# Half of the p products moved ahead of the first norm of a two-layer decoder kernel

## The chip, the cores and the metric

The kernel runs on one core of a Trainium2 chip. The metric is the device time of one execution in microseconds (us). TensorE (PE) does the matrix products, VectorE (DVE) and ScalarE (ACT) the elementwise work, GpSimd (POOL) small work, masks and some DMAs, SyncE (SP) issues the other DMAs. Every engine works through its own instructions in the order in which the program lists them.

## The reference

Two layers over 512 positions of 1024 channels, in float32. Each layer computes, with its own weights:

```python
h = rmsnorm(x, g_pre)
proj = h @ w_in                       # queries, keys, values, gates and merge logits of four mixers
o = four causal mixers(proj)          # sparse attention, gated convolution, stick-breaking, spatial gating
z = (o * silu(gate_paths)) @ w_branch
y = sum(sigmoid(merge_logits + b_merge) * z) @ w_out
x = x + rmsnorm(y, g_post)
x = x + (p[i] @ w_ple) * sigmoid(x @ w_ple_gate)
```

The input p[i] is 512 x 256 and w_ple 256 x 1024. The product of p with w_ple depends on inputs only. The sparse attention turns its queries and keys by rotary tables, cosines and sines of the positions, which the kernel makes once.

## The kernel before

**Products.** A float32 operand is split in two float32r halves, high (a copy on ScalarE) and low (a subtraction on VectorE), and each product is three of TensorE: high by high, high by low, low by high (`mm3`, lines 266 to 271). Weights come in 180 chunks of 128 x 1024 (some 128 x 840) in the order of use (`chunk_plan`). SP loads a chunk into one of three `raw` buffers; `split_chunk` (239) makes `wh` on ScalarE and `wl` on VectorE, in one of six pairs of buffers; then it lists the load of the chunk three further on, so that SP stops there until VectorE has freed a buffer.

**Order.** There is no automatic order: the program lists all instructions. After the start it goes in steps (`step`, 315). Each step lists the elementwise work that follows from the last ones (generators in `front`, `back`, `idle`), the splits that are due (`split_steps`, 165: up to four steps ahead of the use, as the buffers allow), and then one batch of products, mostly 24 of 512 columns. So VectorE and ScalarE work on earlier results while TensorE multiplies.

**The start** is written out by hand as the string `START` (160). For each of four tiles t of 128 positions: `s` sums the squares of x (ScalarE), `h` scales it (two small sums on VectorE, the power -1/2 on POOL, then two scalings on VectorE), `t` transposes it (eight `htr` on TensorE), `e` splits it (`hh` on ScalarE, `hl` on VectorE). `w` splits the next weight chunk, and `mtc` is the six products of tile t with chunk c of the first group, T1 (queries and keys). T1 has 96 such products. Then come the rotary tables (`make_tables`, 387), the masks, the split of two more chunks, and the steps: four `cc` steps, in whose midst the rotary work on T1 (634 to 639), its transposes `qktr` and their splits (`qT`, `kT`, 653 to 661) stand; then the `tp` products (CV), of 256 columns, of which a step has 48.

**The end of a layer.** `Y0` and `Y1` are the products with w_out. `project(0)` multiplies p with the first 512 columns of w_ple (24 products, four PSUM banks, copied out by ScalarE with a factor 0.5, 1196 to 1202), G0 are the products with the first half of w_ple_gate; `project(1)` and G1 are the second half. `use_g` (1222) applies the gate: tanh on ScalarE, then VectorE with the `ple` tile. In layer 0, the use of G1 also makes the next layer's h: it needs the row `gpre`, which takes the one buffer of the rows (347, 1263), and its transposes `htr` follow the step after.

**The memory.** PSUM has eight banks, SBUF tiles of 128 x 512 come from a pool of 25 (`T`, 194).

Of the kernel before, what the change touches and what calls it, by code (L numbers as in the profile page):

```python
# [11 lines left out]
F32 = mybir.dt.float32  # L12
F32R = mybir.dt.float32r
I32 = mybir.dt.int32
AF = mybir.ActivationFunctionType
ALU = mybir.AluOpType

L = 2
# [54 lines left out]
def chunk_plan():  # L73

    plan, step = [], 0
    for l in range(L):
        here = []

        def tgroup(name, cols, steps):
            nonlocal step  # L80
            n = tiles_of(cols)
            for c in range(KT // n):
                first, last = step, step + steps - 1
                if name in PAIRED and (l, name) != (0, "T1"):
                    first, last = step + c // 2, step + c // 2 + 2
                here.append(("t", n * cols, (name, c), first, last))
            step += steps

        def ccols(*names):
            nonlocal step  # L90
            for a in names:
                here.append(("c", KT * P, a, step, step))
                step += 1

        def both(n):
            return [(n, 0), (n, 1)]

        tgroup("T1", 512, 4)
        ccols(*both("cq"), *both("ck"))
        tgroup("CV", 256, 2)  # L100
        tgroup("T2", 420, 4)
        for c in range(2):
            ccols(("bc", c), ("bx", c), ("bb", c))
        ccols(*both("du"))
        tgroup("DV", 256, 2)
        for n in MERGES:
            ccols(*both(f"gate{n}"))
        for n in MERGES:
            for h in range(2):
                here.append(("w", 1024, (n, h), step, step + 3))  # L110
                ccols(*((f"merge{n}", dt) for dt in range(4 * h, 4 * h + 4)))
        for h in range(2):
            tgroup(f"Y{h}", 512, 4)
        for h in range(2):
            here.append(("p", 1024, h, step, step))
            step += 1
            tgroup(f"G{h}", 512, 4)
        plan.append(here)
    return plan
# [5 lines left out]
def lay_weights(w_in, w_branch, w_out, w_ple, w_ple_gate):  # L125
    parts = []

    def rows_in(a):

        return a.reshape(-1, P, a.shape[1]).transpose(1, 0, 2).reshape(P, -1)  # L130

    for l in range(L):
        for kind, n, arg, _, _ in PLAN[l]:
            if kind == "t":
                g, c = arg
                h = slice(512 * int(g[1]), 512 * int(g[1]) + 512) if g[0] in "YG" else None
                src = w_in[l][:, TGROUPS[g]] if h is None else (w_out if g[0] == "Y" else w_ple_gate)[l][:, h]
                r = P * tiles_of(src.shape[1])
                a = rows_in(src[r * c:r * c + r])
            elif kind == "c":  # L140
                g, c = arg
                cols = CCOLS[arg] if arg in CCOLS else _span("merge", D * int(g[5]) + P * c, P)
                a = rows_in(w_in[l][:, cols])
            elif kind == "w":
                a = rows_in(w_branch[l][arg[0]][:, 512 * arg[1]:512 * arg[1] + 512])
            else:
                a = rows_in(w_ple[l][:, 512 * arg:512 * arg + 512])
            assert a.shape == (P, n)
            parts.append(np.ascontiguousarray(a).reshape(-1))
    return np.concatenate(parts)  # L150
# [6 lines left out]
STICKD, SELECT0, ATTEND0, RATES = 3, 8, 5, (1, 2, 3, 2)  # L157


START = ("s0 h0 t0 w e0 m00 s1 h1 w t1 m01 e1 s2 h2 m10,11 t2 w e2 s3 h3 m02,12,20,21 t3 w e3 "  # L160
         "m22,03,13,23,30,31,32,33")
HOP, PE, STEP, SUMS = "hop", "pe", "step", "sums"


# [16 lines left out]
def hybrid_kernel(ctx: ExitStack, tc: tile.TileContext, w, x, p_t, pos, inv_freq, rows, small, ws_t, b_sp, out):  # L181
# [12 lines left out]
    def T(name, shape=(P, 512), dt=F32):  # L194
        return tpool.tile(list(shape), dt, tag="t", name=name)
# [21 lines left out]
    def bank(name):  # L217
        return psum.tile([P, 512], F32, tag="ps", name=name)

    def load(dst, src):  # L220
        nc.sync.dma_start(dst, src)
        return dst
# [8 lines left out]
    def load_to(i):  # L231
        while state["load"] < min(i, len(chunks)):
            k = state["load"]
            n = chunks[k][1]
            raws[k] = stream.tile([P, 1024], F32, tag="raw", name=f"raw{k}", bufs=RAWB)
            load(raws[k][:, :n], bass.AP(tensor=w.tensor, offset=w.offset + offs[k], ap=[[n, P], [1, n]]))
            state["load"] += 1

    def split_chunk(k):
        n = chunks[k][1]  # L240
        h = stream.tile([P, 1024], F32R, tag="wh", name=f"wh{k}", bufs=WB)
        lo = stream.tile([P, 1024], F32R, tag="wl", name=f"wl{k}", bufs=WB)
        halves[k] = (h, lo)
        load_to(k + 1)
        r = raws.pop(k)
        A.copy(h[:, :n], r[:, :n])  # L246
        yield HOP
        V.tensor_tensor(lo[:, :n], r[:, :n], h[:, :n].bitcast(F32), op=ALU.subtract)  # L248
        load_to(k + 1 + RAWB)

    def due(late):
# [7 lines left out]
    def take(n=1):  # L259
        k = state["use"]  # L260
        state["use"] += n
        for c in chunks[k:k + n]:
            assert c[3] <= state["step"] + n
        return list(range(k, k + n))

    def mm3(ps, a, b, start, stop):

        (ah, al), (bh, bl) = a, b
        nc.tensor.matmul(ps, ah, bh, start=start, stop=False)  # L269
        nc.tensor.matmul(ps, ah, bl, start=False, stop=False)  # L270
        nc.tensor.matmul(ps, al, bh, start=False, stop=stop)  # L271
# [15 lines left out]
    def split(h, lo, src, scale=None):  # L287
        half_h(h, src, scale)
        yield HOP
        half_l(h, lo, src, scale)  # L290
# [52 lines left out]
    def load_x(t):  # L343
        for hf in range(2):
            xin[t, hf] = load(T(f"x0_{t}_{hf}"), x[t * P:(t + 1) * P, hf * 512:(hf + 1) * 512])
# [5 lines left out]

    line = spool.tile([1, D], F32, tag="row", name="line", bufs=1)
    load(line, bass.AP(tensor=rows.tensor, offset=rows.offset, ap=[[0, 1], [1, D]]))
    load_x(0)
    lift = consts.tile([1, P], F32, name="lift")
    V.memset(lift, 1.0)
    gpre = [bank(f"gpre{k}") for k in range(2)]
    for k in range(2):
        nc.tensor.matmul(gpre[k], lift, line[:, 512 * k:512 * k + 512], start=True, stop=True)
    load_to(1)  # L360
    prms = [load(consts.tile([P, 40], F32, name=f"prm{l}"), small[l]) for l in range(L)]
    for k in range(1, NT):
        load_to(k)
        load_x(k)
    posi = consts.tile([P, NT], I32, name="posi")
    nc.gpsimd.dma_start(posi, pos)
    freq = consts.tile([P, 48], F32, name="freq")
# [180 lines left out]

    xdram = dram.tile([S, D], F32, name="xdram")


    new_hT()

# [23 lines left out]
    def split_next(n=1):  # L577
        for _ in range(n):
            for _ in split_chunk(state["split"]):
                pass  # L580
            state["split"] += 1


    banks = [bank("tg") for _ in range(NT)]
    take(4)

    def some(*tcs):
        for t, c in tcs:
            h, lo = halves[c]
            for i in range(2):  # L590
                kt, s = 2 * c + i, slice(512 * i, 512 * i + 512)
                mm3(banks[t], hlhs(kt, t), (h[:, s], lo[:, s]), kt == 0, kt == KT - 1)

    gs = [first(t) for t in range(NT)]
    for o in START.split():
        if o[0] == "w":
            split_next()
        elif o[0] == "m":
            some(*((int(i[0]), int(i[1])) for i in o[1:].split(",")))
        else:  # L600
            run_to(gs[int(o[1])], {"s": SUMS, "h": PE, "t": STEP, "e": None}[o[0]])
    make_tables()
    make_masks()
    for prm in prms:
        V.tensor_scalar(prm[:, 8:40], prm[:, 8:40], 0.5, None, op0=ALU.mult)
# [5 lines left out]
    for l in range(L):  # L611
# [566 lines left out]
        tgroup(mlhs, 512, use_y1, 1)  # L1178


        def project(hf):

            k, = take()
            banks = [bank("ple") for _ in range(NT)]

            def mm():
                h, lo = halves[k]
                for t in range(NT):
                    s = slice(t * P, (t + 1) * P)
                    for i in range(2):  # L1190
                        cs = slice(512 * i, 512 * i + 512)
                        mm3(banks[t], (pts[i][0][:, s], pts[i][1][:, s]), (h[:, cs], lo[:, cs]), i == 0, i == 1)

            step(mm)

            def use():
                for t in range(NT):
                    ple[t, hf] = T("ple")
                    A.mul(ple[t, hf], banks[t], 0.5)
                    yield HOP  # L1200

            front.append(use())
# [19 lines left out]
        def use_g(hf, t, ps):  # L1222
# [34 lines left out]
            yield HOP  # L1257
            yield from split_turned(hT, t, tr, 6)

        for hf in range(2):  # L1260
            project(hf)
            if hf and more:
                nxt["gpre"] = row(l + 1, 0, "gpre")
                new_hT()
            tgroup(xlhs, 512, lambda t, ps, hf=hf: use_g(hf, t, ps), None if hf else 0, finish if hf and not more else None)
# [36 lines left out]
```

## Time and profile before

| | |
|---|---|
| median of three runs | 1103.71 us (1101.8, 1103.71, 1104.79) |
| the profiled execution | 1104.97 us, its span 1103.3 us |
| PE | 1088.5 us busy, 5300 products |
| DVE | 771.8 us |
| ACT | 492.3 us |
| POOL | 23.0 us |
| HBM | 103.91 MB read, 4.19 MB written |

The profile is of one execution; all times of its rows count from the first instruction. Busy times are sums over instructions, and products are pipelined: a product of 512 columns is shown 0.39 us long at TensorE's upper clock, though one starts every 0.23 us. A wait is told as the idle time of an engine and the instruction that ended it. "L269" is line 269 of the kernel; the three lines of `mm3` are 269 to 271.

### The profile page before, as it was taken

The page shows a single profiled execution, that of the slowest core. Times are in us where ns is not written, and L with a number is a line of the kernel's source. Part 1 is how long each engine was busy: PE and PEld are TensorE (multiplying, and loading weights), DVE is VectorE, ACT ScalarE, POOL GpSimd, SP SyncE. Part 2 cuts the span into 40 slices and gives each one's busy share as a digit, 9 for nine tenths or more (in the row PEclk, how much of TensorE's full clock was granted, in tenths as well). Part 3 has the DMA queues.
Part 4 walks back from the last instruction along what each step waited for, and adds up shares of the span by engine and source line. Part 5 has one row for each costly group of instructions (what it writes and reads, how often), then busy time and mean ns, then how long its engine had stood idle before and what let it go on. Part 6 is the DMA issues. An engine that isn't in the chain of part 4 may idle for free.

```text
span 1103.3 us, 14018 instructions
## 1 busy us (share of the span) xinstructions
PE 1088.5 (99%) x5300; PEld 923.3 (84%) x5300; DVE 771.8 (70%) x1450; ACT 492.3 (45%) x857; POOL 23.0 (2%) x46
## 2 busy tenths in 40 slices
PE   7989999999999999999999999999999999999998
PEld 5879889888888888888788998988888888888887
DVE  5878778966888754446588688698678877554562
ACT  4557654324423533335436576534243254333351
POOL 2000001000000000000000000000000000000000
PEclk9989999999999999999999999999999999999999
DMA  5223232232323223552441322313222322336331
GB/s 193 78 82 96 76 99 79 80 93 77 96 93 97 73 82 98 177 164 86 143 133 52 108 77 77 101 58 115 77 96 77 97 75 77 96 96 226 99 115 38
DMA packets 34349, 109.01 MB, mean 99 GB/s; under 512 B 4057, under 2 KB 4841, under 8 KB 34282
## 3 DMA queue, kind: packets, MB, share of 16 engines
q1 hardware_dynamic: 34218, 108.10, 30.9%
q8 instruction: 41, 0.67, 0.3%
q14 instruction: 26, 0.21, 0.1%
q0 software_dynamic: 64, 0.03, 0.1%
HBM read 103.91 MB, written 4.19 MB: 98 GB/s over the span
## 4 chain that ended last, share of the span: by engine, by line
PE 93%; DVE 4%; DMA 1%; issue 1%; ACT 1%; SPq 0%; POOL 0%; DVEq 0%; ACTq 0%
PE mg L269 11%; PE mg L271 11%; PE mg L270 11%; PE tg L269 7%; PE tg L271 7%; PE tg L270 7%; PE cc L269 6%; PE cc L270 6%; PE cc L271 6%; PE z L270 3%; PE z L269 3%; PE z L271 3%; PE tp L270 2%; PE tp L271 1%; PE tp L269 1%; PE cs L721 1%
## 5 line engine op out<-in xcount | busy, mean ns | idle before, releaser
L248 DVE TENSOR_TENSOR wl<-raw,wh 128x1024 fp32r<-128x1024 f32 (+1 forms) x180 | 217.2, 1211 | 19.7 <-ACT wh L246 19.0
L269 PE MATMUL mg<-hh,wh 128*128 128x512 f32 x512 | 199.7, 390 | 0.0
L271 PE MATMUL mg<-hh,wl 128*128 128x512 f32 x512 | 199.4, 389 | 0.0
L270 PE MATMUL mg<-hl,wh 128*128 128x512 f32 x512 | 199.3, 389 | 0.0
L246 ACT CAST wh<-raw 128x1024 fp32r<-128x1024 f32 (+1 forms) x180 | 185.5, 1039 | 10.9 <-DMA raw<-in_w 4.3
L1089 ACT ACTIVATE g<-mg,prm 128x512 f32<-128x512 f32 x64 | 44.1, 690 | 227.6 <-PE mg L271 227.6
L269 PE MATMUL cc<-hh,wh 128*128 128x512 f32 x320 | 125.4, 392 | 0.0
L271 PE MATMUL cc<-hh,wl 128*128 128x512 f32 x320 | 124.9, 390 | 0.0
L270 PE MATMUL cc<-hl,wh 128*128 128x512 f32 x320 | 124.8, 390 | 0.0
L271 PEld LDWEIGHTS mg<-hh,wl 128*128 128x128 f32 x512 | 96.1, 188 | 20.3
L270 PEld LDWEIGHTS mg<-hl,wh 128*128 128x128 f32 x512 | 96.2, 188 | 19.7
L269 PEld LDWEIGHTS mg<-hh,wh 128*128 128x128 f32 x512 | 96.1, 188 | 19.6
L1095 DVE SCALAR_TENSOR_TENSOR g<-g,z 128x512 f32<-128x512 f32 x48 | 32.9, 686 | 72.1 <-PE z L271 72.0
L271 PEld LDWEIGHTS cc<-hh,wl 128*128 128x128 f32 x320 | 60.1, 188 | 13.0 <-DVE wl L248 0.3
L270 PEld LDWEIGHTS cc<-hl,wh 128*128 128x128 f32 x320 | 60.2, 188 | 11.7
L269 PEld LDWEIGHTS cc<-hh,wh 128*128 128x128 f32 x320 | 60.1, 188 | 11.6
L869 DVE MAX8 m<-cur 128x8 f32<-128x256 f32 (+2 forms) x96 | 53.6, 559 | 4.4 <-POOL cur L861 2.6
L870 DVE MATCH_REPLACE8 cur<-m,cur 128x256 f32<-128x256 f32 (+2 forms) x96 | 52.1, 542 | 0.0
L269 PE MATMUL tg<-wh,xh 128*128 128x512 f32 (+1 forms) x136 | 51.8, 381 | 0.0
L271 PE MATMUL tg<-wh,xl 128*128 128x512 f32 (+1 forms) x136 | 51.3, 377 | 0.0
L270 PE MATMUL tg<-wl,xh 128*128 128x512 f32 (+1 forms) x136 | 51.2, 377 | 0.0
L269 PE MATMUL tg<-wh,mh 128*128 128x512 f32 x128 | 50.0, 390 | 0.0
(249 smaller groups left out, 2027.6 us busy)
## 6 DMA issues: line engine op xcount, KB each, us to landing
raw<-in_w SPq DMA_DIRECT2D x172, 512.0 KB, 3.6
raw<-in_w SPq DMA_DIRECT2D x8, 420.0 KB, 3.2
x<-in_x SPq DMA_DIRECT2D x8, 256.0 KB, 6.9
res<-in_x SPq DMA_DIRECT2D x8, 256.0 KB, 4.5
xdram<-res SPq DMA_DIRECT2D x8, 256.0 KB, 3.3
res<-xdram SPq DMA_DIRECT2D x8, 256.0 KB, 5.7
out<-res SPq DMA_DIRECT2D x7, 256.0 KB, 2.2
gpost<-in_rows SPq DMA_DIRECT2D x2, 512.0 KB, 5.4
```

The costliest lines, as they stand in the source:

```text
L246: A.copy(h[:, :n], r[:, :n])
L248: V.tensor_tensor(lo[:, :n], r[:, :n], h[:, :n].bitcast(F32), op=ALU.subtract)
L269: nc.tensor.matmul(ps, ah, bh, start=start, stop=False)
L270: nc.tensor.matmul(ps, ah, bl, start=False, stop=False)
L271: nc.tensor.matmul(ps, al, bh, start=False, stop=stop)
L721: nc.tensor.matmul(ps[:, (i - first) * P:], tri if i == own else ones, sh[u][q][:, ci:ci + S - i * P], start=(i == blocks[0] and q == 0), ...
L869: V.max(m8, cur[:, :n])
L870: V.match_replace(cur[:, :n], m8, cur[:, :n], TAKEN)
L1089: A.activation(g, ps, AF.Tanh, bias=b_merge(n, dt), scale=0.5)
L1095: V.scalar_tensor_tensor(g, g, 1.0, z, op0=ALU.add, op1=ALU.mult)
```

## The change

The second half of p times w_ple, of both layers, is computed in the start and written to memory (`pdram`) by POOL's DMAs. `START` has new letters: `pl` splits p of layer l, `Plt` is the six products of tile t for layer l in a PSUM bank, `Elt` copies it out with the factor 0.5 and writes it, `T` makes the rotary tables, which stood behind the start before. The two chunks of weights for it head the list of chunks; the first is loaded and split in two halves. The loads of x now stand behind those of p. In the layers `project` has only the first half left, and ahead of G1 four DMAs of POOL read the second half back. `load_p` (1168) still loads and splits p in each layer.

```diff
@@ chunk_plan
+        if l == 0:
+            here = [("p", 1024, (k, 1), 0, 0) for k in range(L)]
...
+        here.append(("p", 1024, (l, 0), step, step))
+        step += 1
         for h in range(2):
-            here.append(("p", 1024, h, step, step))
-            step += 1
             tgroup(f"G{h}", 512, 4)
@@
-START = ("s0 h0 t0 w e0 m00 s1 h1 w t1 m01 e1 s2 h2 m10,11 t2 w e2 s3 h3 m02,12,20,21 t3 w e3 "
-         "m22,03,13,23,30,31,32,33")
+START = ("p0 w s0 P00 h0 P01 E00 s1 p1 w P02 E01 t0 h1 P03 E02 s2 e0 P10 T t1 E03 w P11 h2 E10 s3 e1 P12 E11 t2 w h3 "
+         "P13 E12 e2 m00,10 t3 E13 e3 m01,11 w m20,21 m30,31 w m02,12,22,32 m03,13,23,33")
@@ load_to, split_chunk: chunk 0 in two halves of its columns
-        A.copy(h[:, :n], r[:, :n])
-        yield HOP
-        V.tensor_tensor(lo[:, :n], r[:, :n], h[:, :n].bitcast(F32), op=ALU.subtract)
+        for c in (slice(0, n // 2), slice(n // 2, n)) if k == 0 else (slice(0, n),):
+            A.copy(h[:, c], r[:, c])
+            yield HOP
+            V.tensor_tensor(lo[:, c], r[:, c], h[:, c].bitcast(F32), op=ALU.subtract)
@@ the first loads
-    load_x(0)
...
+    praw[0] = [load(T("praw"), p_t[0, :, 0])]
     load_to(1)
+    praw[0].append(load(T("praw"), p_t[0, :, 1]))
+    load_x(0)
+    load_x(1)
+    load_pt(1)
+    load_to(2)
+    load_x(2)
+    load_x(3)
+    load_to(3)
     prms = [load(consts.tile([P, 40], F32, name=f"prm{l}"), small[l]) for l in range(L)]
-    for k in range(1, NT):
-        load_to(k)
-        load_x(k)
@@ the start
+    def split_p(l):
+        pts[l] = [(T("ph", dt=F32R), T("pl", dt=F32R)) for _ in range(2)]
+        for q, pr in zip(pts[l], praw.pop(l)):
+            for _ in split(q[0], q[1], pr):
+                pass
+    def ple_mm(ps, pts, k, t):
+        h, lo = halves[k]
+        s = slice(t * P, (t + 1) * P)
+        for i in range(2):
+            cs = slice(512 * i, 512 * i + 512)
+            mm3(ps, (pts[i][0][:, s], pts[i][1][:, s]), (h[:, cs], lo[:, cs]), i == 0, i == 1)
+    def ple_out(l, t):
+        o = T("ple")
+        A.mul(o, pps.pop((l, t)), 0.5)
+        nc.gpsimd.dma_start(pdram[l * S + t * P:l * S + (t + 1) * P, :], o)
...
-    make_tables()
     make_masks()
@@ the end of a layer
+        project()
         for hf in range(2):
-            project(hf)
+            if hf:
+                for t in range(NT):
+                    ple[t, 1] = T("ple")
+                    nc.gpsimd.dma_start(ple[t, 1], pdram[l * S + t * P:l * S + (t + 1) * P, :])
             if hf and more:
                 nxt["gpre"] = row(l + 1, 0, "gpre")
                 new_hT()
```

## Rows read from the trace of the kernel before

**Rows 1.** The page's busy times: us, share of the span, instructions.
```profile
PE 1088.5 (99%) x5300; PEld 923.3 (84%) x5300; DVE 771.8 (70%) x1450; ACT 492.3 (45%) x857; POOL 23.0 (2%) x46
```
**Rows 2.** Waits of PE over the run: us in total, times, longest.
```profile
PE tp L270 <- DVE wl L248: 3.8, 1, 3.8
...
PE htr L455 <- DVE h L1252: 1.1, 1, 1.1
```
**Rows 3.** Timeline of PE in the start: start, length, instruction, idle before.
```profile
11.16 0.79 PE L269 MATMUL tg<-wh,hh 128*128 128x512 f32 x1 [0.49 <-ACT hh L277]
...
13.13 0.63 PE L269 MATMUL tg<-wh,hh 128*128 128x512 f32 x1
13.55 0.63 PE L270 MATMUL tg<-wl,hh 128*128 128x512 f32 x1
...
39.70 0.39 PE L269 MATMUL cc<-hh,wh 128*128 128x512 f32 x1
```
**Rows 4.** Timeline of PE: the second project step's first product, and the one after it.
```profile
531.87 0.39 PE L269 MATMUL ple<-wh,ph 128*128 128x512 f32 x1
...
537.31 0.39 PE L269 MATMUL tg<-wh,xh 128*128 128x512 f32 x1
```
**Rows 5.** The chain that ended last, in the start: start, length, what.
```profile
2.10 7.45 DMA raw<-in_w
...
21.76 0.87 PE htr L455 x8
```
**Rows 6.** Timeline of PE: the wait in `tp`, and the end of its first step.
```profile
67.51 0.58 PE L270 MATMUL tp<-wl,hh 128*128 128x256 f32 x1 [3.78 <-DVE wl L248]
...
75.70 0.28 PE L705 MATMUL cz<-cq,ck 128*128 128x256 f32 x1
```
**Rows 7.** Windows: length, busy us by engine, then granted clock, DMA share, GB/s.
```profile
63.70:67.50 3.80, 0.03 (x1) 0.00 (x0) 3.73 (x6) 3.29 (x4) 0.00 (x0) 0.82 0.00 0
67.50:72.90 5.40, 5.39 (x24) 5.35 (x25) 5.00 (x6) 0.00 (x0) 0.00 (x0) 0.50 0.49 159
```
**Rows 8.** Timeline of DVE and ACT: a scaling, the tables' first instruction, load, what follows.
```profile
25.39 0.75 DVE L566 SCALAR_TENSOR_TENSOR h<-x,rs,gpre 128x512 f32<-128x512 f32 x1 [0.66 <-POOL rs L449]
...
30.39 0.16 DVE L389 CAST posf<-posi 128x4 f32<-128x4 int32 x1
...
33.74 1.28 ACT L406 ACT_TABLE_LOAD   x1 [4.10 <-DVE ang L404]
...
37.21 0.22 DVE L421 CAST ones<-one 128x128 fp32r<-128x128 f32 x1
```
**Rows 9.** Timeline of DVE and ACT from the rotary products to the `tp` chunks.
```profile
39.92 0.69 DVE L634 TENSOR_TENSOR qkr<-tg,cos 128x512 f32<-128x512 f32 x1
...
45.78 0.38 ACT L279 ACTIVATE qT<-qktr 64x256 fp32r<-64x256 f32 x1 [6.45 <-PE qktr L455]
...
49.13 0.42 DVE L285 SCALAR_TENSOR_TENSOR qT<-qktr,qT 64x256 fp32r<-64x256 f32 x1
...
66.24 1.21 DVE L248 TENSOR_TENSOR wl<-raw,wh 128x1024 fp32r<-128x1024 f32 x1
...
68.91 1.23 DVE L248 TENSOR_TENSOR wl<-raw,wh 128x1024 fp32r<-128x1024 f32 x1
```
**Rows 10.** Groups by line and shape: busy us, mean ns of one, idle before.
```profile
L248 DVE TENSOR_TENSOR wl<-raw,wh 128x1024 fp32r<-128x1024 f32 x172 | 209.0, 1219 | 19.6 <-ACT wh L246 19.0
...
L246 ACT CAST wh<-raw 128x1024 fp32r<-128x1024 f32 x172 | 178.4, 1045 | 10.8 <-DMA raw<-in_w 4.3 <-issue 3.5 <-PE tg L271 2.8
...
L283 DVE TENSOR_TENSOR hl<-htr,hh 128x512 fp32r<-128x512 f32 x16 | 10.4, 685 | 2.2 <-ACT hh L277 2.2
```
**Rows 11.** Timeline of SP's queue and DVE between the layers.
```profile
538.62 0.42 SPq L221 DMA_DIRECT2D gpre<-in_rows  x1
...
545.20 0.69 DVE L1228 TENSOR_TENSOR h<-res,gpre 128x512 f32<-128x512 f32 x1 [4.29 <-DMA gpre<-in_rows]
```
**Rows 12.** DMA issues in the first 50 us: KB each, us to landing.
```profile
freq<-in_inv_freq POOLq DMA_DIRECT2D x1, 24.0 KB, 6.7
```

More of the change, by code (lines that the diff above doesn't have):

```diff
@@ L146, in lay_weights @@
             else:
-                a = rows_in(w_ple[l][:, 512 * arg:512 * arg + 512])
+                a = rows_in(w_ple[arg[0]][:, 512 * arg[1]:512 * arg[1] + 512])
             assert a.shape == (P, n)
@@ L235, in load_to @@
             raws[k] = stream.tile([P, 1024], F32, tag="raw", name=f"raw{k}", bufs=RAWB)
-            load(raws[k][:, :n], bass.AP(tensor=w.tensor, offset=w.offset + offs[k], ap=[[n, P], [1, n]]))
+            for c in ((0, n // 2), (n // 2, n)) if k == 0 else ((0, n),):
+                src = bass.AP(tensor=w.tensor, offset=w.offset + offs[k] + c[0], ap=[[n, P], [1, c[1] - c[0]]])
+                load(raws[k][:, c[0]:c[1]], src)
             state["load"] += 1
@@ L359, in hybrid_kernel, with load_pt @@
         nc.tensor.matmul(gpre[k], lift, line[:, 512 * k:512 * k + 512], start=True, stop=True)
+    praw = {}
+    def load_pt(l):
+        praw[l] = [load(T("praw"), p_t[l, :, k]) for k in range(2)]
+    praw[0] = [load(T("praw"), p_t[0, :, 0])]
     load_to(1)
+    praw[0].append(load(T("praw"), p_t[0, :, 1]))
[6 more added lines that the diff above has]
+    load_to(3)
     prms = [load(consts.tile([P, 40], F32, name=f"prm{l}"), small[l]) for l in range(L)]
-    for k in range(1, NT):
-        load_to(k)
-        load_x(k)
     posi = consts.tile([P, NT], I32, name="posi")
@@ L549, in hybrid_kernel @@
     xdram = dram.tile([S, D], F32, name="xdram")
+    pdram = dram.tile([L * S, 512], F32, name="pdram")
     new_hT()
@@ L581, in split_next @@
             state["split"] += 1
-    banks = [bank("tg") for _ in range(NT)]
-    take(4)
+    banks = {}
+    take(6)
+    pts, pps = {}, {}
+    def split_p(l):
[13 more added lines that the diff above has]
+        nc.gpsimd.dma_start(pdram[l * S + t * P:l * S + (t + 1) * P, :], o)
     def some(*tcs):
         for t, c in tcs:
-            h, lo = halves[c]
+            h, lo = halves[2 + c]
+            if t not in banks:
+                banks[t] = bank("tg")
             for i in range(2):
@@ L595, in hybrid_kernel @@
     for o in START.split():
-        if o[0] == "w":
+        if o == "w":
             split_next()
+        elif o == "T":
+            make_tables()
+        elif o[0] == "p":
+            split_p(int(o[1]))
+        elif o[0] == "P":
+            l, t = int(o[1]), int(o[2])
+            pps[l, t] = bank("ple")
+            ple_mm(pps[l, t], pts[l], l, t)
+        elif o[0] == "E":
+            ple_out(int(o[1]), int(o[2]))
         elif o[0] == "m":
@@ L1178, in hybrid_kernel, with project @@
         tgroup(mlhs, 512, use_y1, 1)
-        def project(hf):
+        def project():
             k, = take()
@@ L1186, in mm @@
             def mm():
-                h, lo = halves[k]
                 for t in range(NT):
[L1189 to L1192, printed above, removed]
+                    ple_mm(banks[t], pts, k, t)
             step(mm)
@@ L1197, in use @@
                 for t in range(NT):
-                    ple[t, hf] = T("ple")
-                    A.mul(ple[t, hf], banks[t], 0.5)
+                    ple[t, 0] = T("ple")
+                    A.mul(ple[t, 0], banks[t], 0.5)
                     yield HOP
```

## The prediction

> **What bounds the kernel now.** I read the page's busy times first: TensorE works in 99% of the span [rows 1], so a change helps only where it removes work of TensorE, its idle time, or time at its lower clock. The waits by engine come next, and they leave few such places [rows 2]: one wait of 3.8 us in the first layer, before the `tp` products, and one of 1.1 us before the `htr` transposes between the layers. What is left stands at the start, in TensorE's timeline [rows 3]: the first product of the first group (T1) comes at 11.16 us, products of 512 columns follow each other every 0.42 us there (13.13 to 13.55, TensorE's lower level, 1.2 GHz), and the group ends at 39.70, where the first `cc` product begins. At the upper level, 2.4 GHz, such a product takes 0.2267 us: the 24 of one `project` step run from 531.87 to 537.31 [rows 4]. T1's 96 products would need 21.8 us at that rate and its 32 transposes 3.5 (0.87 for eight [rows 5]), so some 14 us of the first 39.7 are start-up. That is the room the moved products could fill.
>
> The wait before `tp` costs twice. TensorE stands still for 3.78 us until VectorE has made a `wl` [rows 6]; the granted clock falls in that wait (mean 0.82) and stays at 0.50 through 67.5 to 72.9 [rows 7], 5.4 us of work at half rate, so 2.7 us more. VectorE is late there because it was busy with the rotary tables from 30.39 to 37.21 [rows 8] and began the rotary products only at 39.92 [rows 9].
>
> **The change part by part.**
>
> *Removed later.* Each layer loses one `project` step of 24 products. Both stand where TensorE never waits, so they come off the end in full: 2 x 5.44 = **-10.9 us** [rows 4]. The four copies out of PSUM that go with each (half a `wh` copy each, 0.5 us, [rows 10]) lay on ScalarE, which is not the bound there: 0.
>
> *The start.* I place the new order by hand, engine by engine, with the durations of [rows 8, 10]. Two things differ from before: the norm's x tiles are now asked for behind four loads of 256 KB (two of p, two halves of the weight chunk), and `split_p` copies both halves of p before the weights, so ScalarE stops at the fourth load. Before, the first MB (x tile 0 and the first chunk) had landed at 9.55 [rows 5]; the fourth load closes the same MB a little earlier in the queue, and I take 9.2 (7 to 10.5: it moves all that follows by some 0.6 us for each us). Then:
>
> - ScalarE: p 9.2 to 9.7, the weight halves to 10.7. TensorE's first product: 10.4, as late as before.
> - ScalarE goes on with four square sums, the first copy out (after its products, 13.5), two copies of p for layer 1 and `wh1`, to 17.4; VectorE's `wl1` follows to 18.6, h1 (its sums and POOL's power some 0.8, then twice 0.7, [rows 8]) to 21.0, two `hl` (0.6 apart, [rows 10]) to 22.1.
> - Now VectorE's queue has T, the tables: 6.8 us from first to last [rows 8], to 28.9, with ScalarE blocked between the sine and the cosine (to 28.3). Queued behind on ScalarE: the copy E03 and `wh2`, to 29.8; on VectorE: `wl2` to 31.0 and then the sums and scaling of h2, 0.8 and 0.75, to 32.7.
> - TensorE meanwhile has P00 to P12, 42 products, and 16 transposes: 9.5 + 1.7 us at the upper level, 2.7 more for the stretch at the lower one (5.4 us of it, as in [rows 7]; before, it was 7.2 with gaps between), so it is through at 24.3 and its next instruction, t2, waits for h2: **8.4 us idle**. P13 and every product of T1 stand behind t2 in its queue, so the waiting products cover nothing.
> - From 32.7: 102 products (23.1), 16 transposes (1.7) and, since 3.8 us idle brought the clock down before [rows 6, 7], 2.7 for the lower level again: T1 ends at **60.2** against 39.70, **+20.5**. Bounds: 16.5 (load at 7, the clock holding) and 23.5 (load at 10.5, 7.2 us at the lower level, a second table load of 1.3).
>
> So 48 products cost 20.5 us in front to save 10.9 behind.
>
> On tables the Trainium skill ("ScalarE: Activation LUTs", What ACT_TABLE_LOAD costs, and Table sets: the hidden batching unit) says to batch activations by set, since each switch costs a load and a drain, 2.66 us, and names copy and identity but not the square among the functions that every set has. The new order puts the sine between the square sums of tiles 2 and 3. By that rule T would take 1.4 longer and the square might ask for another 2.7; the sum would be up to 4 us higher. The trace does not agree on the drain: the load took 1.28 us, and VectorE waited for the whole trip within the 6.8 of [rows 8]. Whether the square survives a sine no run here shows yet; the sum goes without both.
>
> *What else is issued there.* Eight writes to memory go on POOL, each behind its copy out, and h1, h2 and h3's powers stand behind them. An issue took 0.54 us for `freq` (I allow up to 1.5); h2's power waits for VectorE until 31.5 and E03's write is issued by 29.5: 0, and if all were 1 us later, +1. On SP, the loads of x for tiles 2 and 3 and the chunks land before ScalarE asks for them at the places above; the masks on POOL end before their first use at 76: 0. Both p are also loaded and split again in the layers: that work stays as it was.
>
> *The wait before `tp`.* VectorE finishes the tables, all `hl` and both `wl` ahead of the `cc` steps at about 48, well before 60.2, so it takes T1's banks as they close. Bank 0 closes 4.1 us (18 products) before the end of T1. Before, rotary work began 0.2 us after that end; the 9.2 us of work to 49.13 [rows 9] can now begin 3.9 before it. But the next, `qT`, needs the transposes behind the first `cc` step, and ScalarE's copy of them starts 6.1 after T1's end (45.78), so VectorE goes on there at 6.5 instead of 9.43: a lead of 2.9, which nothing later widens (VectorE has no wait up to 66.24). The first `wl` for `tp` is ready 24.9 after T1's end instead of 27.8, the second 2.67 later, at 27.6. Of the step's 48 products 12 use the first; 36 of 256 columns, 0.12 each (half of 0.2267 and a little), remain: `cz` follows at 31.95 instead of 36.0 [rows 6]. **-4.05**; at least 2.9 (the lead), at most 6.5 (wait and clock all gone). Late next is the second `wl`, 1.3 us.
>
> *Between the layers.* The next norm's row, `gpre`, was issued at 538.62, in SP's order behind the stores and weight loads of the second `project` step; VectorE waited for it to 545.20 [rows 11]. The new order issues it before the step that follows the last G0 product, behind only the loads of the two chunks split in G0's last step: I put it near 529.5 and the landing (6.55 us, 538.62 to about 545.2) at 536, before the first G1 tile is through at 536.9. The transposes' wait goes: **-1.1** (0 to 1.1). The four reads back per layer on POOL have to land by 537.6, 6 us into G1; POOL has nothing else to do in G0, and a small load on that queue landed after 6.7 us [rows 12], so issued by 530 they are in time: 0, or up to +2.
>
> Sum: 20.5 - 10.9 - 4.05 - 1.1 = **+4.45 us**. The profiled execution took 1104.97 (span 1103.3 and 1.7 around it): 1109.4. It stands 1.3 above the median of the three runs, 1103.71; from that it is 1108.2. I take **1108.5**. A measurement here can tell about 0.3%, 3.3 us, from no change: 1100.4 to 1107.0.
>
> **The rivals.**
>
> 1. *The cover holds.* If h2 is ready when TensorE comes to t2 (about 24), TensorE works through from 10.4: 144 products (32.6), 32 transposes (3.5), 2.7 for the lower level: T1 ends at 49.2, +9.5, and the whole is -6.5: **1097** on the median, faster. It is one mechanism: VectorE and ScalarE get through T, `wh2`, `wl2` and h2 before TensorE has used up P00 to P12; each us by which they beat 32.7 is a us back. For it: VectorE has idle time in front that the tables could fill. Against: the 6.8 us of [rows 8] contain two trips to ScalarE, and both queues are in order. Chance 0.14.
> 2. *A smaller price.* The clock does not fall in the wait (-2.7) and the wait before `tp` goes with all that hung on it (-2.45 more): -0.7 on the median, **1103**. For it: 1.1 us idle between the layers left no mark on TensorE's pace. Against: 8.4 is twice the 3.78 that did. Chance 0.20, with an early first MB.
> 3. *No relief before `tp`.* If T1's banks come too late for VectorE to gain its lead, the 4.05 stay: +8.5, **1112**. Against: 12 us of slack on VectorE. Chance 0.08.
> 4. *The change doesn't do what it says:* the reads back land late and hold G1 and the next norm, +1.5 and no gain between the layers: +7, **1111**. Against: POOL is idle there. Chance 0.06.
>
> **How the numbers follow.** The forecast has 0.52; one seventh of it lies under 1107. Faster: 0.14, rival 1. Same: 0.20 + 0.08 = 0.28. Slower: 0.44 + 0.08 + 0.06 = 0.58. The bounds of the terms reach from 1101.7 on the median (16.5 - 10.9 - 6.5 - 1.1) to 1113.4 (23.5 - 10.9 - 2.9 - 0); I give 1100 to 1113, which takes in rivals 2 to 4 and leaves out rival 1.
>
> **What would show it.** TensorE: first `ple` product near 10, a wait of 7 to 9 us before the third `htr` group put down to h, the lower clock after it, first `cc` near 60. VectorE: tables from 22 to 29, idle before the first rotary product. The wait before `tp` under 1.5 us in each of two pieces, clock unbroken; no wait of VectorE for `gpre`. It is wrong if TensorE's wait for t2 is under 4 us, or if the first `cc` comes before 55.

## The result, and the profile after

The changed kernel takes 1111.4 us (four runs, 1111.26 to 1111.71), the kernel before 1104.25 beside it (1101.8 to 1105.05): a ratio of 1.0069, interval 1.0051 to 1.0086. It is slower, as forecast, by 7.15 us where the sum said 4.45. The profiled execution took 1111.26, its span 1109.6: 6.3 more than the span before. The other 0.9 is between the profiled executions and the medians: the one before took 0.72 us more than its median, this one 0.14 less.

First the page's busy times and its HBM line, then TensorE's waits over the whole run (us in total, times, longest).

```profile
PE 1087.6 (98%) x5300; PEld 922.6 (83%) x5300; DVE 774.6 (70%) x1455; ACT 494.9 (45%) x862; POOL 31.8 (3%) x62
...
HBM read 107.06 MB, written 6.29 MB: 102 GB/s over the span
```

```profile
PE htr L472 <- DVE h L585: 7.1, 2, 6.7
PE ple L276 <- ACT wh L253: 5.3, 1, 5.3
PE tp L277 <- DVE wl L255: 2.7, 1, 2.7
```

TensorE has as many products as before and no more busy time [rows 1]; the difference is waiting. The 1.1 us between the layers [rows 2] are gone, the wait before `tp` is shorter, and a wait of 6.7 us for `h` is new. The further bytes are those of the change: 2.10 MB written and read back, and 1.05 MB for p, which is loaded once more. The timeline of TensorE shows where each stands:

```profile
11.47 0.80 PE L276 MATMUL ple<-wh,ph 128*128 128x512 f32 x1 [5.32 <-ACT wh L253]
...
32.66 0.66 PE L472 MATMUL htr<-ident,h 128*128 128x128 f32 x2 [6.74 <-DVE h L585]
...
60.50 0.39 PE L276 MATMUL cc<-hh,wh 128*128 128x512 f32 x1
...
87.04 0.58 PE L277 MATMUL tp<-wl,hh 128*128 128x256 f32 x1 [2.72 <-DVE wl L255]
94.11 0.28 PE L754 MATMUL cz<-cq,ck 128*128 128x256 f32 x1
```

T1 ends at 60.50 against 39.70 [rows 3], **+20.80**. From there to `cz` it takes 33.61 instead of 36.00 [rows 3, 6], **-2.39**. With -1.1 between the layers and -10.88 for the two `project` steps [rows 4] that is +6.43; the span has +6.3. The last two terms can be seen on their own: from `cz` to the end of the span it takes 1015.5 us instead of 1027.6, -12.1. In windows (length, busy us by engine, then granted clock, DMA share, GB/s) the clock follows the new wait, as it followed the old one [rows 7]:

```profile
26.00:32.60 6.60, 0.00 (x0) 0.00 (x0) 4.78 (x18) 5.17 (x12) 1.64 (x3) 0.69 0.20 61
32.70:36.00 3.30, 3.30 (x12) 3.01 (x13) 3.03 (x6) 2.52 (x5) 0.69 (x2) 0.50 0.68 264
36.00:40.00 4.00, 4.00 (x13) 3.09 (x13) 2.60 (x4) 0.60 (x1) 2.71 (x8) 0.66 0.76 260
40.00:44.00 4.00, 4.00 (x24) 3.37 (x23) 2.03 (x3) 2.80 (x4) 1.41 (x5) 1.00 0.02 6
86.00:90.00 4.00, 2.96 (x13) 2.92 (x14) 3.89 (x5) 1.62 (x2) 0.00 (x0) 0.57 0.34 108
```

Why `h` was late is in the timeline of VectorE and ScalarE: the table load, the tables' first instruction, their last (the copies of the cosine, at 28.67), what was queued behind (`wh`, `wl`, a square sum), and then h2's scaling, for which t2 waits.

```profile
21.80 1.28 ACT L423 ACT_TABLE_LOAD   x1
...
23.35 0.16 DVE L406 CAST posf<-posi 128x4 f32<-128x4 int32 x1
...
28.54 1.03 ACT L253 CAST wh<-raw 128x1024 fp32r<-128x1024 f32 x1
...
28.67 0.29 DVE L433 COPY cos<-cs 128x64 f32<-128x64 f32 x2
...
29.60 1.23 DVE L255 TENSOR_TENSOR wl<-raw,wh 128x1024 fp32r<-128x1024 f32 x1 [0.65 <-ACT wh L253]
...
29.96 0.63 ACT L500 ACTIVATE junk<-x 128x512 f32<-128x512 f32 x1
...
31.77 1.41 DVE L585 SCALAR_TENSOR_TENSOR h<-x,rs,gpre 128x512 f32<-128x512 f32 x2 [0.68 <-POOL rs L466]
```

And the relief before `tp`, on VectorE and ScalarE: the first rotary product, ScalarE's first and last copies of the first tile, VectorE's first `qT`, the `wl` that `tp` waits for (before: [rows 9]).

```profile
56.62 0.69 DVE L683 TENSOR_TENSOR qkr<-tg,cos 128x512 f32<-128x512 f32 x1 [6.47 <-PE tg L278]
...
66.58 0.38 ACT L286 ACTIVATE qT<-qktr 64x256 fp32r<-64x256 f32 x1 [15.50 <-PE qktr L472]
...
67.89 0.74 ACT L284 CAST kT<-qktr 64x256 fp32r<-64x256 f32 x2
...
68.66 0.42 DVE L292 SCALAR_TENSOR_TENSOR qT<-qktr,qT 64x256 fp32r<-64x256 f32 x1 [2.85 <-ACT kT L284]
...
85.78 1.21 DVE L255 TENSOR_TENSOR wl<-raw,wh 128x1024 fp32r<-128x1024 f32 x1
```

### The profile page after: what moved, and what is told of

Read it like the earlier page. It is cut to its first block, busy times and chain, and to the rows that moved or that the text cites. A ratio compares the mean times of both kernels' runs of the same rounds, so it can differ in the third digit from the quotient of the medians.

```text
span 1109.6 us, 14091 instructions
## 1 busy us (share of the span) xinstructions
PE 1087.6 (98%) x5300; PEld 922.6 (83%) x5300; DVE 774.6 (70%) x1455; ACT 494.9 (45%) x862; POOL 31.8 (3%) x62
## 4 chain that ended last, share of the span: by engine, by line
PE 95%; DVE 2%; DMA 1%; ACT 1%; issue 1%; SPq 0%; POOL 0%; ACTq 0%
PE mg L276 11%; PE mg L278 10%; PE mg L277 10%; PE tg L276 8%; PE tg L277 8%; PE tg L278 8%; PE cc L276 6%; PE cc L278 6%; PE cc L277 6%; PE z L276 3%; PE z L278 3%; PE z L277 3%; PE tp L277 1%; PE tp L278 1%; PE tp L276 1%; PE cs L770 1%
## 5 line engine op out<-in xcount | busy, mean ns | idle before, releaser
L255 DVE TENSOR_TENSOR wl<-raw,wh 128x1024 fp32r<-128x1024 f32 (+2 forms) x181 | 217.3, 1204 | 20.2 <-ACT wh L253 19.3
L253 ACT CAST wh<-raw 128x1024 fp32r<-128x1024 f32 (+2 forms) x181 | 185.9, 1035 | 13.2 <-DMA raw<-in_w 5.9
```

The costliest lines, as they stand in the source:

```text
L253: A.copy(h[:, c], r[:, c])
L255: V.tensor_tensor(lo[:, c], r[:, c], h[:, c].bitcast(F32), op=ALU.subtract)
```

## The experiments

My theory after the result: the price in front is waiting for VectorE, brought by where the tables stand, with the lower clock behind it; and the relief before `tp` fell short at `qT`. The rivals stand in the expectations.

**e1_tables_late** undoes the tables' place alone.

```
-START = "... E02 s2 e0 P10 T t1 E03 ..."
+START = "... E02 s2 e0 P10 t1 E03 ..."
...
+    make_tables()
     make_masks()
```

> The changed kernel, with the rotary tables made after all of T1's work is issued, as before the change; the moved products stay in front. My theory: TensorE waits 6.74 us at t2 because h2 stands behind the tables in VectorE's queue. Then this wait shrinks to under 1 us, the clock stays up through T1 (3 us of the stretch at half rate saved), the first cc product comes at 51 to 52 instead of 60.50, and the time is 1102 to 1103, a little below the kernel before; the tables end near 43, before T1's first bank closes, so the wait before tp stays near 2.7. Rival A, the wait hangs on the loads or on POOL's writes and not on the tables: first cc near 60, 1111. Rival B, the tables are paid again later: first cc at 51 to 52, but the wait before tp is back at 3.8 or more and the time is 1104 or above.

Measured: 1102.54 us, ratio to the kernel before 0.9988 (0.9979 to 0.9997). TensorE's waits and its first `cc`:

```profile
PE tp L277 <- DVE wl L255: 3.7, 2, 2.7
...
PE htr L472 <- DVE h L585: 0.7, 2, 0.5
```

```profile
51.63 0.39 PE L276 MATMUL cc<-hh,wh 128*128 128x512 f32 x1
```

So 8.9 of the 20.8 us hung on the tables' place: rival A is out. The other 11.9 are little more than the 10.88 of the moved products themselves: taken together, the gaps of the start covered none of them. The wait before `tp` grew from 2.7 to 3.7 us, near the 3.8 that rival B named, but `cz` comes 33.58 after the first `cc`, as in the changed kernel (33.61), and the time is under its 1104, so rival B is out too. After a wait of the same 2.72 us the granted clock stayed at 1.00 in e1 (77 to 84) and fell in the changed kernel (0.57 in 86 to 90), and `cz` came no later for it: the slower products only fill what is a second wait of 0.98 us in e1. This one step turns the loss into a gain of 0.1%.

**e3_one_project** measures the removal alone.

```
-            project(hf)
+            if not hf:
+                project(hf)
```

> The kernel before, with the second project step of each layer and its weight chunk left out, nothing put in front (the second half of the gate uses the first half's products, so its values are not the reference's). This measures the removal alone. My theory: 24 products of 0.2267 us per layer come off in full, 10.9 us, and up to 1.1 us between the layers with them: 1092.2 to 1093.4. Rival, part of these steps covered waits for other engines that now show: 1095 to 1099.

Measured: 1092.26 against 1104.24, ratio 0.9886 (0.9866 to 0.9906): -12.0 (the interval is 10.4 to 14.8), the two steps and the wait between the layers, as expected. Within that interval nothing of it is given back.

**e4_fill and e8_fill18** put products into the new wait whose results nobody reads.

```
+        elif o[0] == "F":
+            ps = bank("fill")
+            for i in range(28):    # e8: 18
+                nc.tensor.matmul(ps, pts[0][0][0][:, 0:P], halves[0][0][:, 0:512], start=True, stop=True)
...
-P12 E11 t2
+P12 E11 F t2
```

> The changed kernel, with 28 products of 512 columns whose results nobody reads put into the wait ahead of t2 (6.35 us at the upper clock, the wait is 6.74). It separates the wait itself from the lower clock after it. My theory: the clock fell because TensorE stood idle, and 6.1 us of T1 then ran at half rate: with the filling it stays at 2.4 GHz, t2 comes at 32.7 as before, the first cc product at 57.4 instead of 60.50, and the time is 1108 to 1108.7. Rival, T1 after the wait is paced by VectorE and ScalarE and not by the clock: first cc within 0.5 of 60.5 and 1111.4; or the filling holds up t2: later than 1111.4.

> e4 with 18 products instead of 28: the filling waits for a PSUM bank to 28.3 and takes 4.1 us, so it ends before h2 is there and cannot hold up t2, as the 28 did by 2.2 us. My theory of the lower clock's share: T1 from t2 on takes 24.8 us instead of 27.84, the first cc product comes near 57.4 and the time is 1108 to 1108.8, against 1111.3. Rival, 18 products leave too much idle time and the clock falls as before: first cc near 60.3 and 1111.

Measured: e4 1110.39 (1.0058, 1.0045 to 1.0071), e8 1111.15 with executions from 1108.22 to 1112.27. The totals missed: the filling itself waits for a PSUM bank, to 28.32 and 28.37, and then holds t2 up (in e8 the clock fell within it). The share of the clock can be read all the same, from t2 to the first `cc`. TensorE in e4:

```profile
28.32 6.65 PE L649 MATMUL fill<-wh,ph 128*128 128x512 f32 x28 [2.68 <-ACT ple L622]
34.81 1.03 PE L472 MATMUL htr<-ident,h 128*128 128x128 f32 x8
...
59.71 0.39 PE L276 MATMUL cc<-hh,wh 128*128 128x512 f32 x1
```

24.90 us there, 24.90 in e8 (34.01 to 58.91), 27.84 in the changed kernel (32.66 to 60.50). TensorE waits for nothing in that stretch in any of the three, and the granted clock is 1.00 from t2 to 42 in both filled runs: the lower clock costs **2.94** of the 20.8.

**e2_transposes_first and e5_ropes_first** go at the wait for `qT`. e2 issues the first tile's transposes ahead of the first `cc` step; e5 does so too, and issues all rotary products ahead of `qT`:

```
         else:
-            for t in range(NT):
-                front.append(later(use_t1(t, t1_banks[t]), t // 2))
+            gens = [use_t1(t, t1_banks[t]) for t in range(NT)]
+            for g in gens:
+                next(g)            # e2: tiles 0 and 1 only
+            next(gens[0])
...
+            front.append(gens[0])
+            for t in range(1, NT):
+                front.append(later(after_mm(gens[t]), t // 2))
```

> The changed kernel, with the transposes of T1's first tile issued ahead of the first cc step instead of behind it; nothing else moves. My theory of the 1.7 us by which the relief before tp fell short: VectorE's lead was spent at qT, where it waited 2.85 us for ScalarE's copies, and these stood behind transposes that TensorE reaches only 5.5 us after T1's end. Then that wait of 2.85 goes, the first wl for tp is ready 2.7 to 2.85 earlier, the wait before tp falls from 2.72 to under 0.3 and the clock stays up: cz at 29 to 30 after the first cc instead of 33.6, and 1107 (1106.5 to 1109 if one of the two stays in part). Rival, VectorE then waits for ScalarE's copies of the next tile instead, or the second wl binds: the wait before tp stays over 2, 1110.5 to 1111.5.

> The changed kernel again with the transposes of T1's first tile ahead of the first cc step, and now all four tiles' rotary products issued ahead of qT on VectorE. In e2 the first qT stood in front of the products of tiles 2 and 3, so VectorE waited there as long as before, only earlier. My theory: VectorE's lead before tp was spent in that one wait; with the rotary products in it the wait is under 0.3, the first wl for tp is ready 2.6 to 2.85 earlier against T1's end, the wait before tp is under 0.3 in each of two pieces and the clock stays up: cz 29 to 31 after the first cc instead of 33.6, and 1107 (1106.5 to 1108.5). Rival: VectorE's work up to the wl is longer in this order or another wait (ScalarE's copies of the next tile) takes the lead: cz over 32.5 after the first cc and 1110 or more.

Measured: e2 1110.14 (1.0061, 1.0046 to 1.0076): the rival came true. There is little gain at that place, `cz` 33.01 after the first `cc` instead of 33.61 (37.25 after the first rotary product instead of 37.49), since `qT` now stood before the other tiles' products and VectorE waited 2.58 for ScalarE all the same. e5 1107.85 (1.0032, 1.0021 to 1.0042). VectorE and TensorE in e5:

```profile
54.30 0.69 DVE L683 TENSOR_TENSOR qkr<-tg,cos 128x512 f32<-128x512 f32 x1 [6.39 <-PE tg L278]
...
66.89 0.42 DVE L292 SCALAR_TENSOR_TENSOR qT<-qktr,qT 64x256 fp32r<-64x256 f32 x1 [0.78 <-ACT kT L284]
```

```profile
58.53 0.48 PE L276 MATMUL cc<-hh,wh 128*128 128x512 f32 x1
...
82.67 0.39 PE L277 MATMUL tp<-wl,hh 128*128 128x256 f32 x1 [0.61 <-DVE wl L255]
85.35 0.39 PE L277 MATMUL tp<-wl,hh 128*128 128x256 f32 x1 [0.99 <-DVE wl L255]
89.65 0.28 PE L764 MATMUL cz<-cq,ck 128*128 128x256 f32 x1
```

`cz` comes 31.12 after the first `cc`, 2.5 earlier than in the changed kernel. Counted from the first rotary product it is 2.14 earlier (35.35 instead of 37.49), since the transposes now lie ahead of `cc`. Three waits stayed larger than the 0.3 that I expected (0.78, 0.61, 0.99). The medians differ by 3.55 us, more than this place shows: in e5's profiled execution the front, which the edit leaves alone, was shorter too (first `ple` product at 10.71, and 26.63 us from t2 to `cc` instead of 27.84). So some 2 of the 3.55 are shown to be the order's.

**e11_before_ropes** puts e5's order into the kernel before.

> The kernel before, with e5's order of the rotary products and the transposes; nothing moved in front. It tests whether that order alone brings the relief before tp, without idle time of VectorE ahead of it. My theory: VectorE is busy up to 39.92 there and has no lead to keep, so the wait before tp stays near 3.8 and the time within 1 us of the kernel before. Rival, the order itself takes the wait away: cz 33.5 or less after the first cc instead of 36.0 and 1102 or less.

Measured: 1103.04 against 1104.0, 0.9991 (0.9982 to 1.0000): within what can be told from no change, but not as I thought. The wait before `tp` did fall, to 1.5, and `cz` came 32.64 after the first `cc`, as the rival had it; but the time did not follow, because the wait moved ahead of `cc`, to the transposes, which wait for the rotary product:

```profile
PE qktr L455 <- DVE qkr L639: 2.2, 1, 2.2
PE tp L270 <- DVE wl L248: 1.5, 2, 1.0
```

All these runs have one thing in common. From VectorE's first rotary product to `cz` it takes, less VectorE's wait for `qT`, 34.5 to 34.7 us: 34.64 in the changed kernel, 34.54 in e1, 34.67 in e2, 34.55 in e4, 34.57 in e5, 34.54 in e11. Only e8 (35.1, the clock at 0.66 in 85 to 90) and the kernel before lie off; there it was 35.78 without such a wait, with the clock at half rate in `tp` [rows 6, 7, 9]. Between the two VectorE's timeline in the changed kernel has no other wait than the one for `qT`. This stretch belongs to VectorE; what moves `cz` is when VectorE begins and whether it waits.

**e6_cover and e7_both** put TensorE's cover in another order: the first half of p and of the weights are split as soon as they land, and the first 12 products use only them; the tables come last. e7 has e5's order as well.

```
+START = ("pa wa Q00 Q10 wb pb Q20 s0 h0 Q30 s1 h1 Q01 Q11 t0 E00 w p1 e0 Q21 E01 t1 Q31 e1 s2 P10 w s3 P11 P12 h2 P13 E10 "
+         "w h3 m00 m10 E11 t2 e2 E12 w m01,11 t3 e3 m20 w m30 m21,31 E02 m02,12,22,32 E03 m03,13,23,33 E13 T")
```

(`pa`, `pb`, `wa`, `wb` split a half; `Q21` is the second half of the products of layer 0's tile 2.)

> The changed kernel with another order in front: the first halves of p and of the weights are split as soon as they have landed and the first 12 products use them alone, layer 1's products stand between the transposes of the tiles, and the tables come after T1's work. My theory: what the moved products cost in front is waiting, not their number. TensorE's first product comes at 6.2 instead of 11.47, no wait in T1 is over 1.5, the first cc product comes at 47 to 48.5 instead of 60.50; the wait before tp is that of e1 (3.7 in two pieces, cz 34.3 after the first cc): 1098 to 1100.5. Rival, the second quarter MB lands late again and the halves bring only a wait after 12 products: first cc 50 to 52, 1101.5 to 1103.5.

> e6's order in front with e5's order of the rotary products and transposes. If both theories hold the two gains add up: first cc at 47 to 48.5, cz 29 to 31 after it, 1094 to 1096.5, faster than both kernels by 8 us or more. If VectorE, later free because T1 ends earlier (its last wl and the masks end near 44), can no longer take T1's banks as they close, the second gain is lost and it is e6's time, 1098 to 1100.5.

Measured: e6 1103.21 (0.9993, 0.9984 to 1.0002), e7 1100.81 (0.9968, 0.9957 to 0.9979). Both lie over what I expected, e6 by 2.7 us and e7 by 4.3: the products begin at 6 to 7, but the first `cc` comes only at 52.18 and 52.51. e6's time is the one that its rival named, but the rival's wait after 12 products is not there; TensorE waits elsewhere. TensorE in e7, and a window of it:

```profile
6.03 0.80 PE L278 MATMUL ple<-wh,ph 128*128 128x512 f32 x1
...
19.88 0.66 PE L474 MATMUL htr<-ident,h 128*128 128x128 f32 x4 [2.88 <-DVE hl L292]
...
52.51 0.48 PE L278 MATMUL cc<-hh,wh 128*128 128x512 f32 x1
```

```profile
22.00:26.00 4.00, 4.00 (x14) 3.16 (x13) 1.93 (x4) 4.00 (x10) 1.08 (x2) 0.71 0.14 43
```

The transposes of the second tile wait for `hl` of the first, whose bank they get, and the clock drops. I had not counted banks.

**e9_order, e10_order_loads and e12_two_tiles** count them: copies out stand ahead of the transposes, the tables in VectorE's gaps. e10 loads the second weight chunk ahead of x and has yet another order of the operations (its string is not shown); e12 is e9 with two tiles' transposes ahead of `cc`. The string of e9 and e12:

```
+START = ("pa wa wb Q30 pb Q00 Q10 s0 Q11 Q01 h0 Q20 s1 t0 E01 p1a h1 Q31 w p1b Q21 e0 P12 E00 s2 P10 h2 w t1 E12 E03 "
+         "s3 w P11 E10 E02 P13 t2 e1 e2 w m00 h3 m20 w m21 m01 m22 E11 t3 m02 T m10 m03 e3 E13 m11 m30 m31 m12 m13 "
+         "m32 m23 m33 M")
```

> e7 with the operations in front in another order. In e7 TensorE still waited 2.88 us before the second tile's transposes, because the PSUM bank that they take was the first tile's and VectorE had not read it yet, and 1.6 us for h; the clock fell after it (0.71 in 22 to 26). VectorE idled 4.8 us between 21.9 and 36.2 and then came to the rotary products only at 48.86. Here copies out free the banks before the transposes, and the tables fill VectorE's gaps. My theory: no wait of TensorE over 2 us before T1's end, first cc near 49 (48 to 50) instead of 52.5, first rotary product near 44 instead of 48.86, cz near 79 instead of 83.61: 1095.5 to 1097.5. Rival: the wait moves to another place once more, first cc 51 to 52.5: 1099 to 1101.

> As e9, and the loads in another order too: the second chunk of weights ahead of x, the tiles of x between the others. My theory: first cc near 48 to 49, cz near 78.5: 1095 to 1097. Rival: x lands too late for the first transposes, TensorE waits over 3 us for h: 1098 or more.

> e9 with the second tile's transposes, too, ahead of the first cc step. In every run so far cz followed VectorE's first rotary product by 34.5 to 34.6 us plus its wait for qT (e7 34.75 with 0.19, e10 35.66 with 1.11, e9 36.28 with 1.74). My theory: that wait of 1.74 goes, cz comes 34.5 to 34.8 after the first rotary product, near 79 if this starts at 44 as in e9, and the time is 1095.8 to 1096.8 against 1097.5. Rival: TensorE waits for the second tile's rotary products ahead of cc, or for tp as long as before: 1097.5 or more.

Measured: e9 1097.54 (0.9941, 0.9925 to 0.9957), e10 1097.21 (0.9938, 0.9924 to 0.9952), e12 1097.19 (0.9944, 0.9930 to 0.9957). All three beat the kernel before, by 6.5 to 6.8 us side by side, and with it the changed kernel (0.994 against its 1.0069). Their times lie 0.04 to 0.4 us over the upper ends that I expected. In e9, TensorE's waits and the rows that decide:

```profile
PE ple L280 <- DVE wl L256: 1.8, 1, 1.8
PE tp L280 <- DVE wl L256: 1.5, 2, 1.0
```

```profile
44.01 0.68 DVE L701 TENSOR_TENSOR qkr<-tg,cos 128x512 f32<-128x512 f32 x1
...
49.27 0.48 PE L279 MATMUL cc<-hh,wh 128*128 128x512 f32 x1
...
57.55 0.42 DVE L295 SCALAR_TENSOR_TENSOR qT<-qktr,qT 64x256 fp32r<-64x256 f32 x1 [1.74 <-ACT kT L287]
...
80.29 0.28 PE L782 MATMUL cz<-cq,ck 128*128 128x256 f32 x1
```

44.01 + 34.54 + 1.74 = 80.29. e12 shows the same sum once more (44.30 + 34.54 + 1.07 = 79.91): there the wait only moved on to the third tile, and I had expected it to go. Between e9, e10 and e12 the runs show no difference.

The gain of e9 lies in the second part more than in the first. Its first `cc` still comes 9.57 us later than in the kernel before (49.27 against 39.70), nearly the 10.88 that the moved products save behind; from there to `cz` it takes 31.02 instead of 36.00. VectorE begins the rotary work 5.26 us ahead of the first `cc`, where it began 0.22 after it before the change. So most of the gain is this head start, and little of it the filling of the start.

## Why the prediction was right, and what was off

- **The project steps, -10.9.** Right: 10.88 in the trace and 12.0 in e3, with the 1.1 between the layers.
- **The start, +20.5.** Right at +20.80, though two parts were off and cancelled, so that the closeness is partly luck. The fourth load landed about 1 us later than the 9.2 I took (ScalarE's copy of it ran at 10.29), so TensorE began at 11.47 instead of 10.4. The tables took 5.6 us (23.35 to 28.96) instead of 6.8, because the table load no longer stood between the angles and the sine; so h2's scaling began at 31.77 and TensorE, through at 25.9, waited 6.74 instead of 8.4. The lower clock, taken as 2.7, cost 2.94 (e4, e8).
- **Rival 1, the cover holds.** This is e1: with the tables elsewhere TensorE waits only 0.7 for h and T1 ends at 51.6. The mechanism was named rightly, and the 6.8 us in VectorE's queue decided against it. Of 49.2, the rival's own end of T1, 2.4 us are missing: 1.0 of the later start (11.38), 0.7 of those waits, the rest not traced.
- **The wait before `tp`, -4.05.** This is the term that was mis-sized: -2.39. The step that failed is the sentence that VectorE goes on at `qT` 6.5 us after T1's end, because ScalarE's copies start at 6.1. They did start there (66.58, 6.08 after). But VectorE's first `qT` ran at 68.66, 8.16 after: 0.03 after the *last* of the tile's six copies had ended. So 1.66 of the lead of 2.9 were lost, and 4.05 - 1.66 is the 2.39 measured. The wait stayed one piece of 2.72, and the clock fell after it (0.57 in 86 to 90), where I had two short pieces and an unbroken clock. e5's order gave the lost part back (2.14). The Trainium skill has a rule that I left out ("PSUM — Partial Sum Buffer", PSUM bank collisions raise a hardware error): two engines must not access one bank in the same quadrant of 32 partitions at the same time, reads against reads included, so accesses have to be kept apart by semaphores. The trace agrees with it, copies first and then `qT`, and so do e1 and e2 (0.03 and 0.04 us after the last copy). But the rule doesn't explain all of it: the first `qT` reads 64 partitions, as do the first three of the six copies, and these had ended at 67.59. By that rule's quadrants VectorE could start then, 1.04 us sooner (an estimate from these rows); that was not tried, and why the wait reaches to the last copy no run shows.
- **Between the layers, -1.1.** Right: no wait is left in TensorE's list, and neither engine waited for `gpre`. The reads back were issued at 531.60 and nothing waited for them (rival 4 is out).
- **POOL, 0.** Right: eight writes of 0.54 to 0.60 us, and h2 waited 0.68 for its power, as long as before (0.66, [rows 8]).
- **Rivals 2 and 3.** The clock did fall (against 2), and the relief came in part (against 3). The changed kernel landed between my sum and rival 3; its median is nearer to the 1112 of rival 3 and the 1111 of rival 4 than to my 1108.5, but the mechanism of neither is in the trace.
- **The table load.** The load took 1.28 us and ran directly behind ScalarE's copies (they end at 21.78, it starts at 21.80), ahead of the angles; in the kernel before it stood behind the angles, and the sine followed 0.02 us after its end (35.04). Square sums of 0.63 us followed the sine at 29.96, and ScalarE's timeline has no further load there. The Trainium skill ("ScalarE: Activation LUTs", What ACT_TABLE_LOAD costs) puts 2.66 us on each switch to another set, load and drain together. No drain shows here on either side of the load, and the second load that the prediction weighed for the square did not come.

## What to carry to other kernels

A product moved into a start-up gap fills it only if the engines that feed the next instruction in the queue stay ahead: work out, for each step of the new order, when VectorE and ScalarE get to it, with everything queued there, and count PSUM banks as you count buffers. Look for the chain that has a constant length in almost every variant (here 34.5 us from VectorE's first rotary product to `cz`) and ask what starts it and what interrupts it; a wait taken away elsewhere only moves. When two engines read the same PSUM tile, plan for the second to start after the last read of the first, as it did in these runs.

## What I had not expected of the hardware

Waits of TensorE of nearly one length end differently: after 2.88 us (e7) the granted clock fell to 0.71 in a stretch of 4 us, after 2.72 (changed kernel) to 0.57, after 2.32 in e8 to 0.57 within the filling, but after 2.68 in e4 and 2.72 in e1 it stayed at 1.00. In e8 executions of one kernel spread over 4 us (1108.2, 1110.2 and 1112.2, mean clock 0.998, 0.996 and 0.995). Of the first four loads of 256 KB, which stand first in every order, the first two came early (ScalarE took them at 3.99 and 5.36 in e7) and the next two late: ScalarE waited for the third until 8.81 (e9) to 9.37 (e7), and where it asked for the fourth first, until 9.52 (e5) to 10.29 (the changed kernel).
